# Half-size buffers for raw weights, later places for the stores of early-made weights, and a wider spread of the early parts

## The chip, the cores and the metric

The kernel runs on one core of a Trainium2 chip. The metric is device time in microseconds (us), the median of three runs. Lower is better. In the trace PE is TensorE, PEld its weight loads, DVE VectorE, ACT ScalarE, POOL GpSimd and SP SyncE, the engine whose queue issues nearly all transfers.

## The reference, cut to what matters

Two layers of a diffusion backbone work on 256 context tokens and 256 latent tokens of width 1024. Layer 0 mixes tokens by retention with four heads, layer 1 by a gated linear recurrence (RG-LRU). Each layer then has a gated convolutional feed-forward block (FFN). All norms are modulated by vectors that come from two large products with `ada_w`.

```python
for i in range(DEPTH):                       # DEPTH = 2
    mod_l = (silu_c @ ada_w[i] + ada_b[i])   # six vectors of 1024 for each sequence
    h_l, h_c = modulate(rmsnorm(x, ...)), modulate(rmsnorm(ctx, ...))
    out_c, out_l = retention_mixer(...) if i == 0 else lru_mixer(...)
    x, ctx = x + g1 * out_l, ctx + cg1 * out_c
    x = x + g2 * conv_ffn(...)               # (silu(conv(h @ w_up)[:2816]) * conv(...)[2816:]) @ w_down
    ...                                      # ctx gets its FFN in layer 0 alone
return rmsnorm(x, final_norm)
```

Everything is float32, and each weight is used once: 1888 blocks of 128 x 128 in all.

## The kernel before, in words

**Blocks, units, pieces.** The weights are packed in the order of use. Eight blocks make a unit (128 x 1024, 512 KB), sixteen make a piece (1 MB). Products are made in three passes of a reduced float format: a weight is split into a rounded part `whi` and a rest `wlo`, and `mm3` (L489) multiplies `whi` by the high part of the data, `whi` by its low part, and `wlo` by the high part (L491, L492, L493). So each unit needs one cast on ACT (L392, `whi`) and one subtraction on DVE (L425, `wlo`) before PE can use it. `prep_units` (L376) writes both into the program one to three units ahead of PE. The engines run their instructions in the written order.

**Retention, first FFN, recurrence, second FFN.** Blocks 0 to 511 belong to the retention (four heads; blocks 96 to 127, 224 to 255 and 352 to 383 hold the queries and keys of heads 1 to 3, with their rotation on DVE), 512 to 1039 to the first FFN (up in 512 to 687 and 784 to 951, down in 688 to 783 and 952 to 1039), 1040 to 1359 to the recurrence and 1360 to 1887 to the second FFN.

**Ada pieces.** 40 pieces of `ada_w` are mixed into the stream ("ada"; eight small ones at the start come another way). Most are multiplied by a column on ACT (`adap`, L548) and summed on POOL (`ada`, L549), up to eight products a piece, four of them at each tick.

**Early parts.** The 20 pieces of the recurrence (blocks 1040 to 1359) are not split when they are used. They are loaded, split and stored to memory during the retention and the first FFN, and the recurrence loads the finished halves. Such a part is made by `pre_piece` (L429): two casts on ACT (L442), two subtractions on DVE (L449, with a copy of 32 rows, L452, for some blocks), and two stores of 1 MB, `keep` (L454 to L456). The steps wait in `preq`, and `tick` (L333) puts one step at a time into the program. A tick comes after each group of products, mostly every eight blocks; the two staged stretches, at the borders of the retention, the first FFN and the recurrence, have none.

`PRE = (160, 40)` (L261) says where the parts lie: the n-th at block 160 + 40 n, rounded down to a piece.

**Buffers and the queue.** Raw pieces go into four buffers of 1 MB (L367). A load (L369) is written into SP's queue when the piece before it is begun. There it waits until the piece that had the buffer is split or multiplied. SP issues in order, so what waits at its head holds up everything behind it, the stores (L456) included. Other intermediate tiles share a pool of 56 buffers of 2 KB a partition (L281).

Of the kernel before, what the change touches and what calls it, by code (L numbers as in the profile page):

```python
# [7 lines left out]
F32 = mybir.dt.float32  # L8
# [4 lines left out]
P = 128  # L13
D = 1024
KD = D // P
NT = 512
# [241 lines left out]
            self.issue(t, e, at)  # L258


PRE = (160, 40)  # L261
BLOCKS, PIECES, KEPT = make_plan()
AH = (2, 3, 3)
DI = (3, 2, 8)
SO, SI, SQ = (0, 6, 1.0)
# [7 lines left out]
class Net:  # L273
    def __init__(self, ctx, tc, wpk, xt, cv, par, cst, out):
        self.tc, self.nc, self.out = tc, tc.nc, out
        self.d_w, self.d_x, self.d_c, self.d_par, self.d_cst = wpk, xt, cv, par, cst
        self.cp = ctx.enter_context(tc.tile_pool(name="cp", bufs=1))
        self.wp = ctx.enter_context(tc.tile_pool(name="wp", bufs=WBUFS))
        self.gp = ctx.enter_context(tc.tile_pool(name="gp", bufs=1))
        self.pp = ctx.enter_context(tc.tile_pool(name="pp", bufs=8, space=bass.MemoryType.PSUM))  # L280
        self.nslot = 56  # L281
        self.uid = 0
        self.raw, self.units = {}, {}
        self.npiece = self.nunit = self.nlo = self.pos = self.npast = 0
# [6 lines left out]
        self.preq = deque()  # L291
# [41 lines left out]
    def tick(self, n=1):  # L333
        self.now += 1
        self.sync()
        ready = [f for t, f in self.due if t <= self.now]
        self.due = [(t, f) for t, f in self.due if t > self.now]
        for f in ready:
            f()
        for _ in range(min(self.ada_rate, len(self.adaq))):  # L340
            self.adaq.popleft()[1]()
        if self.preq:
            self.preq.popleft()[1]()
        for _ in range(min(n, len(self.bg))):
            self.bg.popleft()()
# [4 lines left out]
        self.sync()  # L350


    def load_pieces(self, upto):
        while self.npiece <= min(upto, len(PIECES) - 1):
            i = self.npiece
            if PIECES[i][:2] == ("ada", "k"):
                self.raw[i] = [self.slot(name="ak") for _ in range(4)]
                for j, r in enumerate(self.raw[i]):
                    self.nc.sync.dma_start(r, self.d_w[i, :, j * NT:(j + 1) * NT])
                self.npiece += 1  # L360
                continue
            while self.adaq and self.adaq[0][0] <= i - 4:
# [3 lines left out]
            n = PIECE if PIECES[i][0] != "blk" else min(PIECE, (len(BLOCKS) - PIECES[i][1]) * P)  # L366
# [3 lines left out]
            self.raw[i] = r  # L370
            self.npiece += 1
            if cut < n:
                self.load_pieces(i + 1)
                self.nc.sync.dma_start(r[:, cut:n], self.d_w[i, :, cut:n])

    def prep_units(self, upto):  # L376

# [18 lines left out]
    def unit_hi(self, e):  # L396
        u = self.nunit
        if u in KEPT:
            hi, lo = (self.wp.tile([P, UNIT], F32R, tag=f"w{n}", name=f"w{n}{u}") for n in ("hi", "lo"))
            for j, t in enumerate((hi, lo)):  # L400
                self.nc.sync.dma_start(t.bitcast(F32), self.kept[u][:, j, :])
            self.units[u] = (hi.bitcast(F32), hi, lo)
            self.nunit += 1
            return
        pi = self.piece_of[u // 2]
        self.pass_ada(pi)
        self.load_pieces(pi + 1)
        r = self.raw[pi][:, (u % 2) * UNIT:(u % 2 + 1) * UNIT]
# [20 lines left out]
    def pre_piece(self, pi):  # L429

        nc = self.nc
        self.load_pieces(pi + 1)
        r = self.raw[pi]
        st = {}

        def hi(h, u):
            st[h] = t = self.wp.tile([P, 2, UNIT], F32R, tag="pre", name=f"pre{u}", bufs=2)
            o = 0
            cuts = [(a, n) for kind, a, n in self.runs(u) if kind == "main"] + [(UNIT, UNIT)]
            for a, n in cuts:  # L440
                if a > o:
                    nc.scalar.copy(t[:, 0, o:a], r[:, h * UNIT + o:h * UNIT + a])  # L442
                if n > a:
                    nc.scalar.copy(t[:, 0, a:n].bitcast(F32), r[:, h * UNIT + a:h * UNIT + n])
                o = n

        def lo(h, u):
            t = st[h]
            nc.vector.tensor_tensor(t[:, 1, :], r[:, h * UNIT:(h + 1) * UNIT], t[:, 0, :].bitcast(F32), ALU.subtract)  # L449
# [12 lines left out]

    def runs(self, u):

# [61 lines left out]
    def ada_piece(self, pi):  # L526
        _, name, i, half = PIECES[pi]
        layer, bs = ADA_GROUPS[name]
        self.load_pieces(pi + 1)
        r = self.raw[pi]  # L530
        nc = self.nc
        first, last = (i, half) == (0, 0), (i, half) == (len(bs) - 1, 1)
        if first:
# [6 lines left out]
            acc.update({(i, s): self.slot(name="ada") for s in seqs})  # L540

        def product(s, j):
            w, cs = r[:, j * 512:(j + 1) * 512], self.strip[:, half * 4 + j, 30 + s:31 + s]
            if (half, j) == (0, 0):
                nc.scalar.mul(acc[i, s], w, cs)
            else:
                t = self.slot(name="adap")
                nc.scalar.mul(t, w, cs)  # L548
                nc.gpsimd.tensor_tensor(acc[i, s], acc[i, s], t, ALU.add)  # L549

        if name == "g1":
            for j in range(4):
                nc.tensor.matmul(ps[32 * j:32 * j + 32, :], self.strip[:, half * 4 + j, 30 - 2 * i:62 - 2 * i],
                                 r[:, j * 512:(j + 1) * 512], start=first, stop=last, tile_position=(0, 32 * j))
        else:
            self.adaq.extend((pi, lambda s=s, j=j: product(s, j)) for j in range(4) for s in seqs)

        def total(ns):

            for n in ns:  # L560
                (b, s), j = sums[n], n % 4
                o = 30 - 2 * b - s
                nc.tensor.matmul(ps[32 * j:32 * j + 32, :], self.onehot[:, o:o + 32], acc[b, s],
                                 start=n < 4, stop=n >= len(sums) - 4, tile_position=(0, 32 * j))
        if half and name != "g1":
            done = [n for n, (b, s) in enumerate(sums) if b <= i]
            ready = len(sums) if last else len(done) // 4 * 4
            ns = range(self.ada_sum.get(name, 0), ready)
            self.ada_sum[name] = ready
            if ns:  # L570
                self.adaq.append((pi, lambda: self.after(5, lambda: total(ns))))
        if last:
            rows = self.slot(name="adarow")

# [14 lines left out]
            self.adaq.append((pi, lambda: (self.after(n + 1, down), self.after(n + 3, up))))  # L589

    def need(self, name):

# [114 lines left out]
    def setup(self):  # L707
# [13 lines left out]
        self.load_pieces(1)  # L721
        nc.sync.dma_start(self.par[:, 112:], self.d_par[:, 112:])
        self.load_pieces(10)
# [1034 lines left out]
```

## Time and profile before

| | |
|---|---|
| median of 3 runs | 1257.3 us (1255.05 to 1258.12) |
| the profiled execution | 1258.7 us, its span 1256.9 us |
| PE busy | 1196.5 us (95% of the span), 6760 matmuls |
| DVE, ACT, POOL busy | 887.3, 728.9, 352.6 us |
| bytes moved | 265.3 MB, 211 GB/s over the span |
| the chain that ended last | PE 64%, DVE 14%, ACT 9%, DMA 8% |

Times in the trace start at the span's first instruction. PE counts as busy while a matmul is under way, at whichever clock; the granted clock stands as PEclk in the view by stretches, 1.00 for the full 2.4 GHz and 0.50 for 1.2 GHz. The time of a stretch on PE is therefore read from the number of its matmuls, not from its busy share alone.

### The profile page before, as it was taken

What the parts mean: (1) busy time and instruction counts of PE and PEld (TensorE: products, weight loads), DVE (VectorE), ACT (ScalarE), POOL (GpSimd) and SP (SyncE); (2) the same over time, 40 slices, a digit from 0 to 9 for tenths busy, and PEclk for the clock granted to TensorE, in tenths of its full rate; (3) what the DMA queues carried; (4) which work ended last, traced back from release to release, by engine and by line L of the source; (5) the groups of instructions that cost most, each with busy time, mean ns of one, the idle gap of its engine ahead of it and who ended that gap; (6) DMA issues with size and microseconds to landing.
All of it is one profiled execution on the core that took longest, in us unless ns stands there. A gap on an engine that the chain in (4) does not pass through costs nothing.

```text
span 1256.9 us, 17610 instructions
## 1 busy us (share of the span) xinstructions
PE 1196.5 (95%) x6760; PEld 1014.0 (81%) x6760; DVE 887.3 (71%) x1285; ACT 728.9 (58%) x1098; POOL 352.6 (28%) x242
## 2 busy tenths in 40 slices
PE   8999899989989999988899999899999999999997
PEld 4778688768778888776678887678988889999996
DVE  5655966977595688798864576743757967988843
ACT  5345556656754446767745566532487865766642
POOL 0000546557350021588745344312000001000010
PEclk9999999999999999989999999999999999999999
DMA  9851266656355345576687777622677785455541
GB/s 329 304 186 68 101 248 242 210 217 257 127 205 226 125 186 202 204 264 238 239 326 267 268 268 286 249 101 75 211 279 244 283 306 195 167 177 193 197 140 34
DMA packets 50789, 265.34 MB, mean 211 GB/s; under 512 B 6160, under 2 KB 9872, under 8 KB 25488
## 3 DMA queue, kind: packets, MB, share of 16 engines
q1 hardware_dynamic: 50128, 263.69, 57.4%
q8 instruction: 53, 0.87, 0.3%
q10 hardware_dynamic: 576, 0.52, 0.1%
q14 instruction: 32, 0.26, 0.1%
HBM read 219.62 MB, written 42.99 MB: 209 GB/s over the span
## 4 chain that ended last, share of the span: by engine, by line
PE 64%; DVE 14%; ACT 9%; DMA 8%; issue 3%; SPq 1%; POOL 0%; DVEq 0%; ACTq 0%
PE ps L491 17%; PE ps L493 17%; PE ps L492 17%; DMA raw<-wpk 7%; DVE wlo L425 3%; ACT adap L548 3%; PE ps L915 2%; PE ps L916 2%; PE ps L917 2%; DVE pre L449 2%; ACT whi L392 1%; PE av L492 1%; PE av L491 1%; PE av L493 1%; DVE rstd L648 1%
## 5 line engine op out<-in xcount | busy, mean ns | idle before, releaser
L549 POOL TENSOR_TENSOR ada<-ada,adap 128x512 f32<-128x512 f32 x196 | 312.7, 1619 | 384.9 <-ACT adap L548 356.0
L425 DVE TENSOR_TENSOR wlo<-raw,whi 128x1024 fp32r<-128x1024 f32 x196 | 276.7, 1416 | 31.5 <-ACT whi L392 31.3
L392 ACT CAST whi<-raw 128x1024 fp32r<-128x1024 f32 x196 | 203.4, 1043 | 160.0 <-DMA raw<-wpk 136.5
L493 PE MATMUL ps<-hhi,wlo 128*128 128x512 f32 (+1 forms) x640 | 248.3, 388 | 26.3 <-DVE wlo L425 26.3
L491 PE MATMUL ps<-hhi,whi 128*128 128x512 f32 (+1 forms) x640 | 251.0, 392 | 0.0
L492 PE MATMUL ps<-hlo,whi 128*128 128x512 f32 (+1 forms) x640 | 246.7, 385 | 0.3 <-DVE hlo L667 0.3
L634 POOL TENSOR_TENSOR sq<-sq,sq 128x256 f32<-128x256 f32 x33 | 36.4, 1111 | 496.9 <-ACT sq L628 496.5
L492 PE MATMUL ps<-hx,whi 128*128 128x256 f32 x592 | 168.1, 284 | 0.4 <-DVE hx L667 0.2
L491 PE MATMUL ps<-hx,whi 128*128 128x256 f32 x592 | 168.2, 284 | 0.1
L493 PEld LDWEIGHTS ps<-hhi,wlo 128*128 128x128 f32 x640 | 123.0, 192 | 55.2 <-DVE wlo L425 31.6
L493 PE MATMUL ps<-hx,wlo 128*128 128x256 f32 x592 | 167.5, 283 | 0.0
L491 PEld LDWEIGHTS ps<-hhi,whi 128*128 128x128 f32 x640 | 122.9, 192 | 30.9 <-issue 5.3
L492 PEld LDWEIGHTS ps<-hlo,whi 128*128 128x128 f32 x640 | 123.0, 192 | 24.1 <-issue 1.0
L548 ACT ACTIVATE adap<-raw,strip 128x512 f32<-128x512 f32 x196 | 126.0, 713 | 0.0
L491 PEld LDWEIGHTS ps<-hx,whi 128*128 128x128 f32 x592 | 113.5, 192 | 4.1 <-issue 2.5
L492 PEld LDWEIGHTS ps<-hx,whi 128*128 128x128 f32 x592 | 113.5, 192 | 1.1 <-DVE hx L667 0.8
L493 PEld LDWEIGHTS ps<-hx,wlo 128*128 128x128 f32 x592 | 113.6, 192 | 0.0
L1157 DVE SCALAR_TENSOR_TENSOR cv<-ps,par,cv 128x510 f32<-128x510 f32 (+1 forms) x88 | 53.9, 612 | 74.3 <-ACT cv L1154 74.0
L491 PE MATMUL ps<-fzhi,whi 128*128 128x512 f32 (+1 forms) x198 | 73.6, 372 | 2.2 <-ACT fzhi L513 2.2
L1154 ACT ACTIVATE cv<-ps,par 128x512 f32<-128x512 f32 (+1 forms) x88 | 58.5, 666 | 29.1 <-PE ps L493 29.1
L492 PE MATMUL ps<-fzlo,whi 128*128 128x512 f32 (+1 forms) x198 | 73.1, 369 | 0.2 <-DVE fzlo L514 0.2
L493 PE MATMUL ps<-fzhi,wlo 128*128 128x512 f32 (+1 forms) x198 | 73.1, 369 | 0.0
(204 smaller groups left out, 2298.0 us busy)
## 6 DMA issues: line engine op xcount, KB each, us to landing
raw<-wpk SPq DMA_DIRECT2D x157, 1024.0 KB, 5.9
kept<-pre SPq DMA_DIRECT2D x40, 1024.0 KB, 4.9
whi<-kept SPq DMA_DIRECT2D x40, 512.0 KB, 4.5
wlo<-kept SPq DMA_DIRECT2D x40, 512.0 KB, 5.5
ak<-wpk SPq DMA_DIRECT2D x32, 256.0 KB, 6.5
xc<-xt SPq DMA_DIRECT2D x4, 256.0 KB, 4.0
x<-xt SPq DMA_DIRECT2D x4, 256.0 KB, 5.8
raw<-wpk SPq DMA_DIRECT2D x2, 512.0 KB, 6.1
```

The source lines that it names most:

```text
L392: self.nc.scalar.copy(dst, src)
L425: self.eng(e).tensor_tensor(d[q, o:n], r[q, o:n], hi[q, o:n].bitcast(F32), ALU.subtract)
L449: nc.vector.tensor_tensor(t[:, 1, :], r[:, h * UNIT:(h + 1) * UNIT], t[:, 0, :].bitcast(F32), ALU.subtract)
L491: mm(ps, w[0], x[0], start=start, stop=False)
L492: mm(ps, w[0], x[1], start=False, stop=False)
L493: mm(ps, w[1], x[0], start=False, stop=stop)
L548: nc.scalar.mul(t, w, cs)
L549: nc.gpsimd.tensor_tensor(acc[i, s], acc[i, s], t, ALU.add)
L634: nc.gpsimd.tensor_tensor(self.acc[s], self.acc[s], sq, ALU.add)
L915: mm(pss[t], xh, wh, start=k == 0, stop=False)
L1154: nc.scalar.activation(acc, ps[:, :n], AF.Identity, scale=w(1), bias=self.pc("fcb", layer * 44 + f))
L1157: nc.vector.scalar_tensor_tensor(a3[:, :, 1:], p3[:, :, :NS - 1], w(0), a3[:, :, 1:], ALU.mult, ALU.add)
```

## The change

It has three parts.

1. Raw weights come as halves. `make_loads` lists every load as (piece, half); the pool has `RAWS = 9` buffers of 512 KB in place of four of 1 MB, 4.5 MB for 4 MB. `half` writes loads into SP's queue `AHEAD = 2` halves past the one that is begun. A load waits for the half that stood nine halves earlier. To make room the shared pool shrinks from 56 to 54 buffers.
2. `keep` no longer enters the queue with the next step. It goes to `keepq` with a mark two ticks later, and `tick` takes one from there at a time.
3. `PRE` becomes (64, 48): the n-th early part lies at block 64 + 48 n. The first are at blocks 64, 112, 160 and 208 (before: 160, 192, 240, 272), the last is at 976 (before: 912).

```diff
-PRE = (160, 40)
+PRE = (64, 48)
+RAWS, AHEAD = 9, 2
+def make_loads():
+    loads, place = [], {}
+    for i, p in enumerate(PIECES):
+        if p[:2] == ("ada", "k"):
+            loads.append((i, None))
+        else:
+            loads.extend((i, h) for h in range(2) if p[0] != "blk" or p[1] + 8 * h < len(BLOCKS))
...
+LOADS, PLACE = make_loads()
...
-        self.nslot = 56
+        self.nslot = 54
...
+        if self.keepq and self.keepq[0][0] <= self.now:
+            self.keepq.popleft()[1]()
         if self.preq:
             self.preq.popleft()[1]()
...
-            while self.preq and self.preq[0][0] <= i - 4:
+            while any(t <= n - RAWS for t, _ in self.preq):
                 self.preq.popleft()[1]()
-            r = self.wp.tile([P, PIECE], F32, tag="raw", name=f"raw{i}", bufs=4)
-            cut = n if i > 1 else UNIT
-            self.nc.sync.dma_start(r[:, :cut], self.d_w[i, :, :cut])
...
+            r = self.wp.tile([P, UNIT], F32, tag="raw", name=f"raw{pi}{'ab'[h]}", bufs=RAWS)
+            self.nc.sync.dma_start(r, self.d_w[pi, :, h * UNIT:(h + 1) * UNIT])
+            self.raw[pi, h] = r
+
+    def half(self, pi, h, ahead=AHEAD):
+        self.load(PLACE[pi, h][0] + ahead)
+        return self.raw[pi, h]
...
         def hi(h, u):
+            while len(self.keepq) > 1:
+                self.keepq.popleft()[1]()
...
         def lo(h, u):
...
+            self.keepq.append((self.now + 2, lambda: keep(h, u)))
...
-        self.preq.extend((pi, f) for f in (
-            lambda: hi(0, u), lambda: (lo(0, u), hi(1, u + 1)), lambda: (lo(1, u + 1), keep(0, u)),
-            lambda: keep(1, u + 1)))
+        a, b = (PLACE[pi, h][1] for h in range(2))
+        self.preq.extend([(a, lambda: hi(0, u)), (b, lambda: (lo(0, u), hi(1, u + 1))), (b, lambda: lo(1, u + 1))])
```

Where SP's queue held the two stores of an early part one behind the other, it now has loads between them. This is the part at block 640, in the first FFN; before, its tiles are `pre_4955` and `pre_5005`. Of the loads behind the stores the third, `raw_5125`, is the next piece of blocks.

```order
L369 DMA raw_4916<-wpk 128x2048
L369 DMA raw_5015<-wpk 128x2048
L456 DMA kept_5019<-pre_4955 128x2048
L456 DMA kept_5021<-pre_5005 128x2048
L369 DMA raw_5023<-wpk 128x2048
L369 DMA raw_5121<-wpk 128x2048
L369 DMA raw_5125<-wpk 128x2048
L369 DMA raw_5127<-wpk 128x2048
```

The same part in SP's queue after the change. `raw86` is the next piece of blocks behind the first store, `raw89` the next behind the second.

```order
L394 DMA raw85a<-wpk 128x1024
L394 DMA raw85b<-wpk 128x1024
L482 DMA kept_5264<-pre_5104 128x2048
L394 DMA raw86a<-wpk 128x1024
L394 DMA raw86b<-wpk 128x1024
L394 DMA raw87a<-wpk 128x1024
L482 DMA kept_5323<-pre_5156 128x2048
L394 DMA raw87b<-wpk 128x1024
L394 DMA raw88a<-wpk 128x1024
L394 DMA raw88b<-wpk 128x1024
L394 DMA raw89a<-wpk 128x1024
```

Both stores stand further down, and three half loads stand between them.

How far the weights behind a store are from their use shows on ACT. Before, from the second cast of that part to the cast of the blocks behind its store (`raw_5125`):

```order
L442 CAST pre_5005<-raw_4910 128x1024
L513 CAST fzhi_5007<-cv_4905 128x512
L1154 ACTIVATE cv_5010<-ps_4963,par_89 128x512
L392 CAST whi_5025<-raw_5015 128x1024
...
L392 CAST whi_5073<-raw_5015 128x1024
...
L392 CAST whi_5129<-raw_5125 128x1024
```

After, from the same cast on (`raw86` stands behind the first store, whose cast is eight instructions higher, and `raw89` behind the second):

```order
L467 CAST pre_5156<-raw81b 128x1024
L538 CAST fzhi_5158<-cv_5050 128x512
L1179 ACTIVATE cv_5161<-ps_5112,par_89 128x512
L417 CAST whi_5172<-raw84a 128x1024
...
L417 CAST whi_5224<-raw84b 128x1024
...
L417 CAST whi_5282<-raw86a 128x1024
...
L417 CAST whi_5334<-raw86b 128x1024
...
L417 CAST whi_5392<-raw89a 128x1024
```

Counted on ACT, 17 instructions lay between the cast of a stored half and the first cast behind its store; now it is 25 (first store) and 31 (second store).

On DVE a new part comes into the stretch of head 1's queries and keys (blocks 96 to 127). Before, the split of a unit (`wlo`), the readout of head 0 (`zt`, `zlo`) and the rotation (`ra`, `rb`) alternate:

```order
L425 TENSOR_TENSOR wlo_1194<-raw_1007,whi_1128 128x1024
L514 TENSOR_TENSOR zlo_1167<-zt_1163,zhi_1166 128x512
L976 SCALAR_TENSOR_TENSOR zt_1230<-av_1078,par_89,rstd_1160 128x512
L977 TENSOR_TENSOR zt_1230<-zt_1230,sg_775 128x512
L514 TENSOR_TENSOR zlo_1173<-zt_1169,zhi_1172 128x512
```

After, the second subtraction of the part at block 112 stands between them (the first is a dozen rows higher):

```order
L449 TENSOR_TENSOR wlo_1244<-raw21b,whi_1173 128x1024
L539 TENSOR_TENSOR zlo_1215<-zt_1211,zhi_1214 128x512
L474 TENSOR_TENSOR pre_1209<-raw20b,pre_1209 128x1024
L1001 SCALAR_TENSOR_TENSOR zt_1281<-av_1121,par_89,rstd_1205 128x512
L1002 TENSOR_TENSOR zt_1281<-zt_1281,sg_794 128x512
L539 TENSOR_TENSOR zlo_1221<-zt_1217,zhi_1220 128x512
```

Nothing else in that row of work has changed its place.

## Rows read from the trace of the kernel before

**Rows 1.** Waits of PE, 125 to 812 us: total us, times, longest

```profile
PE ps L493 <- DVE wlo L425: 37.4, 16, 5.2
```

**Rows 2.** View by stretches: length, busy us (instructions) of PE, PEld, DVE, ACT, POOL; PEclk, DMA share, GB/s

```profile
125.00:160.00 35.00, 31.30 (x131) 24.28 (x130) 34.38 (x53) 21.18 (x35) 21.10 (x13) 0.95 0.31 103
...
250.00:280.00 30.00, 24.43 (x100) 19.32 (x99) 21.97 (x36) 15.89 (x25) 13.52 (x9) 0.94 0.59 221
...
344.00:372.00 28.00, 24.30 (x99) 19.36 (x99) 27.27 (x36) 14.85 (x26) 20.26 (x12) 0.94 0.59 215
...
526.00:632.00 106.00, 88.25 (x351) 68.98 (x350) 88.36 (x72) 74.35 (x112) 85.78 (x53) 0.92 0.64 239
632.00:660.00 28.00, 27.24 (x114) 21.25 (x115) 17.20 (x19) 14.48 (x20) 11.55 (x8) 0.94 0.80 314
660.00:775.00 115.00, 114.83 (x508) 93.69 (x507) 72.87 (x87) 67.51 (x94) 53.97 (x35) 1.00 0.72 273
775.00:812.00 37.00, 32.46 (x138) 25.11 (x137) 21.71 (x22) 22.78 (x33) 15.40 (x11) 0.95 0.74 287
```

**Rows 3.** Waits of ACT, 160 to 830 us

```profile
ACT whi L392 <- DMA raw<-wpk: 132.9, 28, 11.3
```

**Rows 4.** Waits of SP's queue, 160 to 830 us

```profile
SPq L456 <- DVE pre L449: 151.1, 25, 24.5
SPq L369 <- ACT adap L548: 134.9, 26, 12.3
SPq L456 <- DVE pre L452: 77.5, 12, 14.0
```

**Rows 5.** Instructions of SP's queue in order of time: start, us from first to last

```profile
539.37 4.14 SPq L456 DMA_DIRECT2D kept<-pre  x2
543.60 3.14 SPq L369 DMA_DIRECT2D raw<-wpk  x3
```

**Rows 6.** Chain of waits, 240 to 275 us: start, us, what

```profile
242.55 0.33 SPq L456
...
243.40 8.96 DMA raw<-wpk
```

**Rows 7.** Waits of ACT in 250:280, 344:372, 526:632 and 775:812

```profile
ACT whi L392 <- DMA raw<-wpk: 14.5, 2, 9.2
...
ACT whi L392 <- DMA raw<-wpk: 2.9, 1, 2.9
...
ACT whi L392 <- DMA raw<-wpk: 19.6, 7, 4.2
...
ACT whi L392 <- DMA raw<-wpk: 13.0, 2, 8.0
```

**Rows 8.** Waits of DVE, 526 to 632 us

```profile
DVE cv L1157 <- ACT cv L1154: 18.1, 5, 5.7
```

**Rows 9.** DVE lines L425, L449, L452: ns least/median/most, first and last start

```profile
L425 DVE TENSOR_TENSOR wlo<-raw,whi x196: 1160/1218/2329, 19.0 to 1233.4; 128x1024 fp32r<-128x1024 f32 x196
...
L449 DVE TENSOR_TENSOR pre<-raw,pre x40: 1211/1222/2354, 160.0 to 791.9; 128x1024 fp32r<-128x1024 f32 x40
...
L452 DVE CAST pre<-pre x16: 278/1250/1377, 263.4 to 640.8; 32x256 fp32r<-32x256 f32 x16
```

**Rows 10.** Issue to landing, L369 (raw loads, 1 MB) and L401 (finished halves, 512 KB)

```profile
DMA to landing us min/median/max: 4.7/5.8/13.9
...
DMA to landing us min/median/max: 3.7/5.2/10.0
```

**Rows 11.** View by stretches, the start and the middle of the recurrence

```profile
0.00:31.40 31.40, 26.64 (x124) 14.62 (x128) 17.55 (x35) 17.25 (x29) 1.68 (x11) 1.00 0.94 329
...
1005.52:1036.90 31.38, 29.58 (x216) 25.92 (x215) 21.91 (x40) 21.82 (x35) 0.00 (x0) 0.99 0.89 305
```

More of the change, by code (lines that the diff above doesn't have):

```diff
@@ L258, in run @@
             self.issue(t, e, at)
-PRE = (160, 40)
+PRE = (64, 48)
+RAWS, AHEAD = 9, 2
 BLOCKS, PIECES, KEPT = make_plan()
+def make_loads():
[5 more added lines that the diff above has]
+            loads.extend((i, h) for h in range(2) if p[0] != "blk" or p[1] + 8 * h < len(BLOCKS))
+    a = loads.index((1, 1))
+    loads.insert(a + 1, loads.pop(a))
+    n = 0
+    for i, (pi, h) in enumerate(loads):
+        place[pi, h] = (i, n)
+        n += h is not None
+    return loads, place
+LOADS, PLACE = make_loads()
 AH = (2, 3, 3)
@@ L350, in flush, with load @@
         self.sync()
[L353 to L360, printed above, removed]
+    def load(self, upto):
+        while self.nload <= min(upto, len(LOADS) - 1):
+            pi, h = LOADS[self.nload]
+            self.nload += 1
+            if h is None:
+                self.raw[pi] = [self.slot(name="ak") for _ in range(4)]
+                for j, r in enumerate(self.raw[pi]):
+                    self.nc.sync.dma_start(r, self.d_w[pi, :, j * NT:(j + 1) * NT])
                 continue
-            while self.adaq and self.adaq[0][0] <= i - 4:
+            n = PLACE[pi, h][1]
+            while any(t <= n - RAWS for t, _ in self.adaq):
                 self.adaq.popleft()[1]()
-            while self.preq and self.preq[0][0] <= i - 4:
+            while any(t <= n - RAWS for t, _ in self.preq):
                 self.preq.popleft()[1]()
-            n = PIECE if PIECES[i][0] != "blk" else min(PIECE, (len(BLOCKS) - PIECES[i][1]) * P)
-            r = self.wp.tile([P, PIECE], F32, tag="raw", name=f"raw{i}", bufs=4)
-            cut = n if i > 1 else UNIT
-            self.nc.sync.dma_start(r[:, :cut], self.d_w[i, :, :cut])
[L370 to L374, printed above, removed]
+            r = self.wp.tile([P, UNIT], F32, tag="raw", name=f"raw{pi}{'ab'[h]}", bufs=RAWS)
[4 more added lines that the diff above has]
+        return self.raw[pi, h]
     def prep_units(self, upto):
@@ L406, in unit_hi @@
         self.pass_ada(pi)
-        self.load_pieces(pi + 1)
-        r = self.raw[pi][:, (u % 2) * UNIT:(u % 2 + 1) * UNIT]
+        r = self.half(pi, u % 2)
         hi = self.wp.tile([P, UNIT], F32R, tag="whi", name=f"whi{u}")
@@ L431, in pre_piece @@
         nc = self.nc
-        self.load_pieces(pi + 1)
-        r = self.raw[pi]
+        rs = [self.half(pi, h) for h in range(2)]
         st = {}
         def hi(h, u):
+            while len(self.keepq) > 1:
+                self.keepq.popleft()[1]()
             st[h] = t = self.wp.tile([P, 2, UNIT], F32R, tag="pre", name=f"pre{u}", bufs=2)
-            o = 0
+            r, o = rs[h], 0
             cuts = [(a, n) for kind, a, n in self.runs(u) if kind == "main"] + [(UNIT, UNIT)]
@@ L528, in ada_piece @@
         layer, bs = ADA_GROUPS[name]
-        self.load_pieces(pi + 1)
-        r = self.raw[pi]
+        rs = [self.half(pi, h) for h in range(2)]
+        places = [PLACE[pi, h][1] for h in range(2)]
         nc = self.nc
@@ L553, in ada_piece @@
                 nc.tensor.matmul(ps[32 * j:32 * j + 32, :], self.strip[:, half * 4 + j, 30 - 2 * i:62 - 2 * i],
-                                 r[:, j * 512:(j + 1) * 512], start=first, stop=last, tile_position=(0, 32 * j))
+                                 rs[j // 2][:, j % 2 * 512:(j % 2 + 1) * 512], start=first, stop=last, tile_position=(0, 32 * j))
         else:
-            self.adaq.extend((pi, lambda s=s, j=j: product(s, j)) for j in range(4) for s in seqs)
+            self.adaq.extend((places[j // 2], lambda s=s, j=j: product(s, j)) for j in range(4) for s in seqs)
         def total(ns):
@@ L570, in ada_piece @@
             if ns:
-                self.adaq.append((pi, lambda: self.after(5, lambda: total(ns))))
+                self.adaq.append((places[1], lambda: self.after(5, lambda: total(ns))))
         if last:
@@ L588, in ada_piece @@
             n = 0 if name == "g1" else 5
-            self.adaq.append((pi, lambda: (self.after(n + 1, down), self.after(n + 3, up))))
+            self.adaq.append((places[1], lambda: (self.after(n + 1, down), self.after(n + 3, up))))
     def need(self, name):
@@ L720, in setup @@
         self.load_const("sel")
-        self.load_pieces(1)
+        self.load(3)
         nc.sync.dma_start(self.par[:, 112:], self.d_par[:, 112:])
-        self.load_pieces(10)
+        self.load(LOADS.index((10, None)))
         self.mod = [self.const([P, 48, 2], name="mod") for _ in range(2)]
```

12 lines of the change are left out of this document (6 added, 6 removed).

## The prediction

> **What bounds the kernel now.** I read the page first: PE is busy for 95% of the span, so a change that adds no matmul can win back only what PE loses. The waits of PE between 125 and 812 us, where raw weights, ada pieces and early parts come together, have one large row: 37.4 us in 16 waits, all for `wlo`, the subtraction on DVE [rows 1]. The reader is to see that PE hardly waits for anything else there.
>
> The view by stretches then tells where, and how much it is worth. From 660 to 775 us PE makes 508 matmuls in 115 us at full clock, 0.226 us each; that is PE's own pace. Six stretches fall short of it [rows 2]. Their matmuls at that pace, taken from their length, leave: 125 to 160, 131 matmuls, 29.7 us, 5.3 lost; 250 to 280, 100, 22.6 us, 7.4 lost; 344 to 372, 99, 22.4 us, 5.6 lost; 526 to 632, 351, 79.5 us, 26.5 lost; 632 to 660, 114, 25.8 us, 2.2 lost; 775 to 812, 138, 31.2 us, 5.8 lost. That is 53 us, more than the 37 us of waits, since the granted clock falls to half for a while around each stall (mean 0.92 to 0.95 in these stretches, 1.00 in the full one).
>
> Next, why `wlo` is late. ACT's waits have 132.9 us in 28 waits for a raw load to land before the cast that `wlo` needs [rows 3]. SP's queue says why those loads start late: for 228 us (151.1 and 77.5) its head is a store that waits for an early part's subtraction or row copy, and for 134.9 us a load whose buffer still waits for ACT's ada products [rows 4]. In order of time the pattern is plain: two stores, and right behind them three loads at once [rows 5]. The chain of waits runs through one such place: the store at 242.55, a load from 243.40 that takes 8.96 us because it shares the DMA engines with the store and its neighbours [rows 6]. A load alone lands in 4.7 us [rows 10].
>
> Not all of the loss is of this kind. From 125 to 160 us DVE is busy for 34.4 of 35 us, from 344 to 372 for 27.3 of 28 [rows 2]: there DVE itself is the limit, and ACT waits for loads only 2.9 us in the second of them [rows 7].
>
> **The change part by part.**
>
> *Later stores.* They remove nothing; 40 stores still pass through SP. But before, 17 ACT instructions lay between the cast of a stored half and the first cast that needs a load behind its store; now 25 and 31. A store waits for a subtraction made about one tick after the cast. In the first FFN a tick is eight blocks, 24 matmuls, 5.4 us at full pace. So the head start of the loads goes from about one tick to two or more, 5 us to 11 us or more, against the 7 to 9 us that a load in such a bunch takes [rows 6, 10]. Its bunch is smaller too: the first piece of blocks behind the stores had two whole pieces ahead of it; now there is none behind the first store, and three halves behind the second. I expect most of ACT's waits for loads behind stores to go.
>
> *Halves.* A load waits for the half nine back instead of the whole piece four back: at least one half more of depth, and an ada piece gives back its first half one tick before its second. The loads gated by ada products (134.9 us of SP's waits) start one to two ticks sooner by this. The price: twice as many loads, each issued in about 0.33 us [rows 6] by a queue that mostly waits, so hidden. What a half costs on the DMA engines no raw load shows; the finished halves that the recurrence loads are of that size. Least time alone is 3.7 us against 4.7 for a whole piece [rows 10], so two halves cost between nothing more, if they overlap fully, and 2 x 3.7 - 4.7 = 2.7 us a piece, if not at all. By carried bytes, the recurrence's halves go at 305 / 0.89 = 343 GB/s of full share [rows 11], whole pieces with stores at 314 / 0.80 = 392 [rows 2], 14% less. At 0.64 to 0.80 share that binds nowhere in the middle; at the start the share is 0.94, and pieces 4 and 8 come there: 0 to 5.4 us; nearest to the measured rates, I take 0.5. The Trainium skill speaks against this edit: its page "DMA: Bandwidth & Descriptors" (Rules for kernel authors) asks for at least 1 MiB a transfer, and by its fixed 2.0 us a transfer (Anatomy of one DMA, measured on another issuing path) each halved piece would take 2 us more; by that rule the 0.5 would be 4 for pieces 4 and 8. The trace agrees for a transfer alone, where half the bytes save only 1 us of 4.7, and not at the rates of full queues.
>
> *54 shared buffers for 56.* No wait of ACT for a POOL sum shows in the trace, so 0; if buffers run out in the first FFN, ACT waits for POOL, which is busy 85.8 of 106 us there [rows 2]: at most that stretch then keeps its length.
>
> *Wider parts.* DVE's sum of work stays. Two things move. In blocks 240 to 288 one part is left where two were, and with them two subtractions and two row copies, 2 x 1.2 + 2 x 1.25 = 5 us by the medians [rows 9], leave DVE in and just before 250 to 280. And the part now at block 112 puts two subtractions into 125 to 160, where DVE is full: 2 x 1.21 to 2 x 2.35 us [rows 9], and PE waits for DVE there, so it is on the path. I take 3.0 (2.4 to 4.7, up to 1.75 more for a clock drop: 5% of 35 us). The part at block 352 has one row copy more than before: +1.25 in 344 to 372, which ACT's 2.9 us there offset: 0 (-3 to +3). In the first FFN's up stretch three parts stay three; only the last slides by a piece.
>
> *Now the gains.* 526 to 632: ACT's 19.6 us of waits for loads [rows 7] stand behind DVE's 18.1 us of waits for ACT [rows 8]. If all go, DVE is next: 88.4 us of work, and at the 97 to 98% that its fullest rows show, 91 us. So between 91 and 106; with a few us of idling left I take 93, a gain of 13. 250 to 280: DVE has only 22.0 us of work and loses 5, PE needs 22.6; 14.5 us of waits for loads [rows 7] go: gain 5.5 of the 7.4 (3 to 7.4). 775 to 812: DVE 21.7, PE 31.2, waits for loads 13.0: gain 5.0 of 5.8 (2 to 5.8). 632 to 660 is the tail of the stretch before: 1 (0 to 2).
>
> *Sum:* +0.5 + 3.0 + 0 - 13 - 5.5 - 5.0 - 1.0 = -21. The profiled execution took 1258.7 us, so 1237.7; it lay 1.4 above the median of 1257.3, so 1236 for the median. With the good ends (0 + 2.4 - 3 - 15.4 - 7.4 - 5.8 - 2 = -31) it is 1226; with the poor ones of the middle terms (2 + 4.7 + 1 - 8 - 4 - 3 = -7) 1250.
>
> **Rivals.**
>
> *VectorE keeps the first FFN.* DVE's subtractions take 2.3 us instead of 1.2 at many places [rows 9], POOL is busy 81% of 526 to 632, and a faster stretch has both at once more often. Then the 13 us and the 1 us stay lost: -7, time 1250. For it: 88 of 106 us busy already. Against: DVE's idle time has ACT, and ACT's has loads, as its releaser [rows 7, 8].
>
> *The stores still stand first.* They still wait for the same subtractions at the head of one queue, and loads behind them are still bunched. If DVE runs a tick late just where parts lie, the second tick is eaten and only the depth gained by halves stays: about -2, time 1255. Against: 25 and 31 instructions for 17.
>
> *Slower: the full DVE stretches grow.* Place: 125 to 160 and 344 to 372. Price: two slowed subtractions 4.7, one copy 1.4, and a further clock drop in each, 1.75 twice: +9.6. It decides as soon as the other stretches give back under 9 us, so when loads after stores stay as late as now; then 1267 less the 1.4: about 1265. For it: both rows are at 97 to 98%. Against: the stretches that follow have room on DVE (22.0 of 30 us, 72.9 of 115 in rows 2).
>
> *Halves overlap badly.* Each pair costs the 2.7 us that the landing times allow at most. Pieces 4 and 8 then add 5.4 at the start, and a load behind a store loses about half of its second tick, so half of the 24.5 us of gains stays lost: 5.4 + 3 - 12 = -4, time 1253. For it: rows 10; against: rows 2 and 11, by bytes. The page's rule of 1 MiB points this way.
>
> *PE at its own pace.* With fewer stalls POOL's and DVE's slow pairs part, and nearly all 53 us but the DVE-full stretches' come back: about 1218.
>
> **How the numbers follow.** Forecast 1236, chance 0.55 (1226 to 1250). VectorE keeps the first FFN, 1250: 0.16. Stores still first, 1255: 0.08. Halves overlap badly, 1253: 0.04. Slower, 1265: 0.10. PE's pace, 1218: 0.07. A measurement of this kernel tells 0.3%, some 3.8 us, from no change: faster is below 1253.5, same up to 1261. From the cases: faster 0.55 + 0.07 + 0.14 + 0.02 + 0.03 = 0.81, same 0.02 + 0.06 + 0.01 + 0.01 = 0.10, slower 0.09. The range that leaves out a tenth on either side is 1220 to 1256.
>
> **What would show it.** Right: ACT's waits for raw loads from 160 to 830 us fall from 133 us to under 50; SP's waits at the stores shrink, and loads no longer follow them three at once; PE's waits for `wlo` fall from 37 to under 22 us; 351 matmuls of the first FFN's up stretch take about 93 us, with DVE at 93% or more; the first stretch around 125 us is some 3 us longer; raw halves land in about 4 us. The forecast is wrong if ACT's waits go and the up stretch still takes over 100 us (first rival), if ACT's waits stay above 100 us (second), or if the early stretches lose more than the later ones give back (third).

## The result, and the profile after

The changed kernel takes 1240.8 us (median of 4 runs, 1239.3 to 1242.0) against 1257.7 us (4 runs, 1255.1 to 1258.9) for the kernel before, timed beside it: a ratio of 0.9868, 95% interval 0.9848 to 0.9888. The forecast was 1236 in 1220 to 1256. The profiled execution took 1242.0 us, its span 1240.2, so 16.7 us less than the one before.

On the page, the busy line has PE at nearly the same busy time in a shorter span, and the line of the chain has DMA at 4% where it had 8, ACT at 3 where it had 9:

```profile
PE 1190.2 (96%) x6760; PEld 1012.2 (82%) x6760; DVE 899.3 (73%) x1285; ACT 730.9 (59%) x1098; POOL 365.5 (29%) x242
...
PE 74%; DVE 15%; DMA 4%; issue 3%; ACT 3%; SPq 1%; POOL 0%; DVEq 0%; ACTq 0%; POOLq 0%
```

PE's waits from 125 to 800 us (total us, times, longest) answer to [rows 1]. The 37.4 us for `wlo` are 20.0 now; two waits that were small have grown, the second and the third row (2.4 and 2.2 us before, shown behind them):

```profile
PE ps L518 <- DVE wlo L449: 20.0, 9, 6.0
PE st L663 <- POOL sq L659: 4.7, 2, 4.1
PE ps L516 <- ACT fzhi L538: 4.1, 1, 4.1
```

```profile
PE st L638 <- POOL sq L634: 2.4, 2, 1.7
PE ps L491 <- ACT fzhi L513: 2.2, 1, 2.2
```

The view by stretches holds the same matmuls as [rows 2], found by their number in the order of PE, so the lengths compare directly (us; busy us of PE, PEld, DVE, ACT, POOL; PEclk, DMA share, GB/s):

```profile
125.14:163.74 38.60, 31.67 (x132) 24.71 (x131) 38.10 (x55) 21.22 (x35) 21.17 (x13) 0.91 0.49 163
...
527.79:622.18 94.39, 82.91 (x351) 65.84 (x349) 92.56 (x72) 69.46 (x104) 86.39 (x50) 0.95 0.75 253
622.18:650.00 27.82, 27.82 (x114) 21.56 (x115) 15.77 (x18) 16.37 (x22) 17.13 (x11) 0.91 0.87 304
650.00:764.38 114.38, 114.38 (x508) 93.88 (x507) 74.72 (x87) 69.30 (x96) 54.50 (x34) 1.00 0.80 278
764.38:794.62 30.24, 30.24 (x137) 24.10 (x136) 24.66 (x26) 18.46 (x26) 15.44 (x9) 1.00 0.72 245
```

The up stretch of the first FFN went from 106 to 94.4 us, and DVE is busy for 98% of it instead of 83%: it has become DVE's stretch. DVE's own work there grew too, from 88.4 to 92.6 us for the same 72 instructions. The last one went from 37 to 30.2 us, all PE. The first one grew from 35 to 38.6 us.

ACT's waits from 160 to 830 us answer to [rows 3]: one row of 132.9 us has become six of one wait each, 17.3 us in all (7.3 + 3.3 + 2.4 + 2.0 + 1.5 + 0.8). The first two:

```profile
ACT whi L417 <- DMA raw29a<-wpk: 7.3, 1, 7.3
ACT whi L417 <- DMA raw96a<-wpk: 3.3, 1, 3.3
```

DVE's waits from 526 to 625 us answer to [rows 8], 18.1 us there. This row is all that is left:

```profile
DVE fzlo L539 <- ACT fzhi L538: 0.8, 1, 0.8
```

SP's queue (160 to 830 us) answers to [rows 4]. The waits at stores, L482, fall from 228.6 to 138.2 us; 19.0 us more now stand at loads that wait for a part's subtraction. The largest row is loads that wait for a buffer which DVE gives back in its normal course:

```profile
SPq L394 <- DVE wlo L449: 297.5, 81, 16.6
SPq L482 <- DVE pre L474: 104.6, 19, 27.6
SPq L394 <- ACT adap L573: 93.8, 43, 11.0
SPq L482 <- DVE pre L477: 33.6, 11, 10.9
SPq L394 <- DVE pre L474: 19.0, 11, 3.6
```

That row was the largest before the change as well, though [rows 4] do not show it:

```profile
SPq L369 <- DVE wlo L425: 223.3, 41, 18.4
```

And the same early part as in [rows 5], in order of time: two stores there and three loads of 1 MB in a bunch behind them. Now each store stands between half-size loads, which go out a few us apart:

```profile
538.17 0.33 SPq L482 DMA_DIRECT2D kept<-pre  x1
538.59 0.38 SPq L394 DMA_DIRECT2D raw79a<-wpk  x1
540.87 0.33 SPq L394 DMA_DIRECT2D raw79b<-wpk  x1
542.64 0.33 SPq L394 DMA_DIRECT2D raw80a<-wpk  x1
543.02 0.42 SPq L482 DMA_DIRECT2D kept<-pre  x1
543.54 0.40 SPq L394 DMA_DIRECT2D raw80b<-wpk  x1
```

Where the 16.7 us lie is read from the start of the same-numbered matmul in the two traces. The table has it for every kernel that ran; a cell is by how much a stretch (named by its times in the kernel before) is longer than before, the last one up to the start of the last matmul. The two kernels with squares to PE have four matmuls more, which are left out of the count.

| kernel, profiled execution | 0-120 | 120-235 | 235-322 | 322-470 | 470-512 | 512-673 | 673-838 | rest | sum |
|---|---|---|---|---|---|---|---|---|---|
| **the change** | +0.1 | +3.6 | -5.7 | +0.7 | +3.1 | -11.8 | -7.4 | +0.7 | -16.7 |
| later stores alone | +0.6 | 0 | -2.0 | +1.5 | 0 | +0.1 | +5.3 | 0 | +5.5 |
| wider parts alone | +7.0 | +7.6 | -5.6 | 0 | +1.6 | +5.8 | -6.8 | -1.5 | +8.0 |
| halves alone | -0.1 | +0.7 | +0.5 | -0.4 | +3.8 | +10.9 | -5.3 | -1.4 | +8.8 |
| stores and wider parts | +0.2 | +2.7 | -5.5 | +1.0 | +0.1 | +1.3 | -7.4 | 0 | -7.6 |
| halves and stores | +2.0 | +0.7 | -3.4 | +0.8 | -0.8 | -6.4 | -7.4 | 0 | -14.5 |
| halves and wider parts | +1.3 | +4.9 | -5.8 | -0.5 | +5.6 | -7.3 | -7.4 | -1.4 | -10.6 |
| the change, ring of eight | -0.5 | +2.7 | -5.5 | +0.8 | +2.9 | -11.4 | -7.4 | 0 | -18.4 |
| the change, part at 96 | -0.2 | +1.4 | -5.7 | +0.7 | +3.0 | -11.8 | -7.4 | +0.1 | -20.0 |
| the change, squares to PE | -0.3 | +3.5 | -5.7 | 0 | -1.4 | -12.7 | -7.4 | +0.1 | -23.7 |
| the change, parts by hand | -0.6 | +0.7 | -5.7 | +0.7 | +1.8 | -24.7 | -7.4 | 0 | -35.1 |
| the same, squares to PE | 0 | +0.8 | -7.3 | 0 | -0.9 | -24.7 | -7.4 | 0 | -39.6 |
| before, parts by hand | +6.6 | +4.8 | -6.9 | 0 | +2.0 | -12.3 | -7.4 | 0 | -13.2 |

### The profile page after: what moved, and what is told of

It is laid out like the page before. It is cut to its first block, busy times and chain, and to the rows that moved or that the text cites. A ratio compares the mean times of both kernels' runs of the same rounds, so it can differ in the third digit from the quotient of the medians.

```text
span 1240.2 us, 17983 instructions
## 1 busy us (share of the span) xinstructions
PE 1190.2 (96%) x6760; PEld 1012.2 (82%) x6760; DVE 899.3 (73%) x1285; ACT 730.9 (59%) x1098; POOL 365.5 (29%) x242
## 3 DMA queue, kind: packets, MB, share of 16 engines
q1 hardware_dynamic: 72736, 263.70, 61.9%
## 4 chain that ended last, share of the span: by engine, by line
PE 74%; DVE 15%; DMA 4%; issue 3%; ACT 3%; SPq 1%; POOL 0%; DVEq 0%; ACTq 0%; POOLq 0%
PE ps L516 21%; PE ps L517 20%; PE ps L518 20%; DVE wlo L449 4%; PE ps L940 2%; PE ps L941 2%; PE ps L942 2%; DVE pre L474 1%; DVE zlo L539 1%; PE av L517 1%; PE av L516 1%; PE av L518 1%; DVE fzlo L539 1%; DVE cv L1182 1%; DVE zt L1001 1%
## 5 line engine op out<-in xcount | busy, mean ns | idle before, releaser
L574 POOL TENSOR_TENSOR ada<-ada,adap 128x512 f32<-128x512 f32 x196 | 323.3, 1674 | 351.3 <-ACT adap L573 212.4
L518 PE MATMUL ps<-hhi,wlo 128*128 128x512 f32 (+1 forms) x640 | 245.8, 384 | 13.3 <-DVE wlo L449 13.3
L659 POOL TENSOR_TENSOR sq<-sq,sq 128x256 f32<-128x256 f32 x33 | 38.7, 1181 | 500.9 <-ACT sq L653 500.4
L516 PEld LDWEIGHTS ps<-hhi,whi 128*128 128x128 f32 x640 | 122.3, 191 | 31.4 <-issue 4.9
L702 DVE SCALAR_TENSOR_TENSOR xc<-ps,mod,xc 128x256 f32<-128x256 f32 x48 | 23.0, 479 | 60.9 <-PE ps L518 60.9
L518 PE MATMUL ps<-zhi,wlo 128*128 128x512 f32 (+1 forms) x152 | 55.9, 368 | 6.7 <-DVE wlo L449 6.7
L517 PE MATMUL ps<-zlo,whi 128*128 128x512 f32 (+1 forms) x152 | 55.7, 366 | 2.6 <-DVE zlo L539 2.6
```

The source lines that it names most:

```text
L516: mm(ps, w[0], x[0], start=start, stop=False)
L517: mm(ps, w[0], x[1], start=False, stop=False)
L518: mm(ps, w[1], x[0], start=False, stop=stop)
L659: nc.gpsimd.tensor_tensor(self.acc[s], self.acc[s], sq, ALU.add)
```

## The experiments

Each was timed beside the kernel before; times are medians, ratios are to the kernel before with their 95% interval.

**Each edit by itself.** Later stores alone, in the whole-piece kernel:

```diff
+        if self.keepq and self.keepq[0][0] <= self.now:      # in tick
+            self.keepq.popleft()[1]()
...
+            self.keepq.append((self.now + 2, lambda: keep(h, u)))   # in lo
```

> The kernel before with the later stores alone (whole pieces in four buffers, 56 shared buffers, parts at 160 + 40 n). Theory (loads held up behind the stores were the loss): ACT's waits for raw loads fall from 133 us to under 70 and the time to about 1246 (-10 to -14), without the +3.6 us that the part at block 112 costs. Rival (the halves do it, by their depth): the time stays at 1255 to 1258.

Measured: 1262.5 us, 1.0042 (1.0028 to 1.0055), 0.4% slower where a gain was expected. SP's waits from 160 to 830 us (total us, times, longest) show what became of the wait; L461 is the store, L371 the load:

```profile
SPq L371 <- ACT adap L552: 176.1, 34, 13.1
SPq L371 <- DVE pre L453: 109.2, 15, 25.8
SPq L461 <- DVE pre L453: 21.8, 6, 11.8
SPq L461 <- DVE pre L456: 10.9, 3, 6.0
```

The waits at stores did collapse, 228.6 to 32.7 us. But the load four pieces behind an early part takes that part's own raw buffer, and that comes back with the part's second subtraction: the event that the store waited for. So 109.2 us of the wait only changed its instruction; the rest came up at other loads, which wait 41 us longer for ada products and 53 us longer for `wlo`. ACT still waits 115.2 us for raw loads. The loss itself lies at 673-838 (+5.3); what makes loads late there was not followed.

Wider parts alone:

```diff
-PRE = (160, 40)
+PRE = (64, 48)
```

> The kernel before with the parts at 64 + 48 n alone. Theory: stores stand where they stood, so ACT's waits for loads stay above 100 us; +3.6 us at 125 us for the part at block 112, some 3 us back near 250 us where two parts become one, so 1256 to 1261. Rival (the spread thins out VectorE's work and that is the gain): 1243 to 1248.

Measured: 1269.4 us, 1.0099 (1.0083 to 1.0114), slower, 8 us above the expected range. It keeps the gains at 235-322 and 673-838. At 120-235 it loses 7.6 us, and the matmuls at 512 to 526 take 24.2 us for 13.8, where ACT waits 15.8 us for two raw loads. It also loses 7 us ahead of 120, where PE (waits from 60 to 125 us) stands still for an ada piece whose load is held up behind the store of the part at block 64:

```profile
PE ada L553 <- DMA raw<-wpk: 4.9, 1, 4.9
```

ACT's waits for raw loads, 160 to 830 us, are 97.7 us, less than the 132.9 before, in a slower kernel: their sum alone does not tell the time.

Halves alone (each store right behind its subtraction, old places):

```diff
-            self.keepq.append((self.now + 2, lambda: keep(h, u)))
+        self.preq.extend([..., (b, lambda: (lo(1, u + 1), keep(0, u))), (b, lambda: keep(1, u + 1))])
```

> The halves alone: nine half buffers, loads two halves ahead, 54 shared buffers; stores follow with the next step as before, parts at 160 + 40 n. Theory: loads still stand behind the stores, but in smaller bunches and one half deeper: 1247 to 1253, ACT's waits for loads 60 to 100 us. Rival (halves by depth do it all): 1241 or less.

Measured: 1268.5 us, 1.0093 (1.0079 to 1.0107), slower. SP in order of time, at the early part at 520 us: the second store holds the queue until 532, all buffers come free meanwhile, and seven halves go out in 5 us:

```profile
521.53 10.99 SPq L481 DMA_DIRECT2D kept<-pre  x2
532.57 0.42 SPq L394 DMA_DIRECT2D raw74a<-wpk  x1
533.04 0.91 SPq L394 DMA_DIRECT2D raw74b<-wpk  x1
534.00 1.02 SPq L394 DMA_DIRECT2D raw75a<-wpk  x1
535.12 0.67 SPq L394 DMA_DIRECT2D raw75b<-wpk  x1
```

ACT's longest wait for a raw load in any of these runs follows (waits of ACT, 500 to 550 us):

```profile
ACT whi L417 <- DMA raw75a<-wpk: 15.8, 1, 15.8
```

With shorter waits for buffers SP reaches the stores sooner and stands there longer: its waits at stores from 160 to 830 us rise to 306.8 us (208.8 and 98.0), while those at loads for `wlo` fall from 223.3 to 126.3. My theory, by which stores alone bring most of the gain and halves some, fell with these runs.

**Two edits at a time.** Stores and wider parts, without halves (the first two diffs above together):

> The change without the halves: later stores and parts at 64 + 48 n, whole pieces in four buffers. Theory: most of the gain is there without halves, 1241 to 1247; what is left to the halves is the loads that wait for ada products. Rival (halves by depth): 1254 or more.

Measured: 1251.7 us, 0.9963 (0.9950 to 0.9975), between the theory's range and the rival's. The places keep their gain (-5.5 and -7.4), and the later stores spare the 7 us at the ada piece; the up stretch does not move (+1.3), and ACT still waits 106.2 us for loads from 160 to 830 us. Halves and stores, with the parts at the old places:

```diff
-PRE = (64, 48)
+PRE = (160, 40)
```

> The changed kernel with its early parts at the places of before (every 40 blocks from block 160); halves in nine buffers and later stores stay. Theory (two gates in series hold the loads: a store at the head of SP's queue that waits for its part's second half, and the ring of raw buffers; each edit alone only moves the wait to the other gate): with both gates wider ACT's waits for raw loads fall from 136 us to below 40 us and the kernel takes 1236 to 1248 us; the parts at the old places keep the losses at 250-280 and 775-812 us of the kernel before, or some of them. Rival (the gain is the places of the parts): over 1252 us, with ACT's waits above 80 us.

Measured: 1243.3 us, 0.9890 (0.9877 to 0.9904); ACT's waits for raw loads are 28.2 us over the whole run (136.5 before), each over 0.3 us counted. At these places that is what two gates in series do: either edit alone costs time, both together gain. Halves and wider parts, each store right behind its subtraction (the third diff above, with the wider places):

> The changed kernel with each store issued where it was before, in the background step right behind its subtraction; halves and the wider spread stay. Theory (two gates): the store gate is still there and halves make SP wait at it no less, so ACT's waits for raw loads stay above 80 us and the kernel takes 1256 to 1272 us. Rival (the nine half buffers and the places of the parts bring the gain, the later stores nothing): 1240 to 1246 us, ACT's waits below 40 us.

Measured: 1247.2 us, 0.9923 (0.9910 to 0.9937), ACT's waits 75.1 us. Here the theory missed: with SP's waits at stores as long as with halves alone (184.0 + 113.8 = 297.8 us), the kernel is 9.5 us faster than before. In the matmuls at 512 to 639 us of the kernel before, ACT's waits for raw loads are 14.6 us against 26.4 with halves alone. That run and this one differ in the places alone, so with halves the wider places are worth 21 us; by which waits, no run separates.

With this run every combination of the three edits has been timed:

| median, us | neither | later stores | halves | both |
|---|---|---|---|---|
| places of before | 1257 | 1262.5 | 1268.5 | 1243.3 |
| wider places | 1269.4 | 1251.7 | 1247.2 | 1240.8 |

At the old places either edit alone costs 5 to 12 us. At the wider places, where the kernel without them is slower, either alone brings some 18 or 22 us, and the second adds 6 to 11. Two gates that have to open together describe the old places only.

**Ring of eight halves**, as many bytes as the four pieces of before:

```diff
-RAWS, AHEAD = 9, 2
+RAWS, AHEAD = 8, 2
...
-        self.nslot = 54
+        self.nslot = 56
```

> The changed kernel with eight half buffers in place of nine, which is as many bytes as the four whole buffers of the kernel before; the two buffers of the general pool that this frees go back to it. It tells whether the gain is the finer steps of the ring or its larger size. Theory (finer steps: a buffer comes back after each half, not after each piece): 1240 to 1245 us, ACT's waits for raw loads below 45 us. Rival (the ninth buffer carries the gain): over 1247 us, ACT's waits above 70 us.

Measured: 1240.9 us, 0.9874 (0.9854 to 0.9894), no difference from nine; ACT's waits for raw loads are 31.4 us over the whole run against 21.5. What halves add to later stores and wider parts (1251.7 to 1240.9) needs no ninth buffer and no more bytes; the ring's finer step carries it, together with how far ahead loads are written, which changed with it.

**The two losses that the change made.** The second early part at block 96 in place of 112 (here and below the places are a list, of which the n-th is the n-th part's):

```diff
-PRE = (64, 48)
+PRE = (64, 96, 160, 208, ...)
```

> The changed kernel with its second early part at block 96 in place of block 112; all other parts stay. Theory (the stretch 125-160 us has no idle VectorE, and the part's two subtractions there make PE's weights late): the stretch returns to the length it had before the change, the wait for the low weights of 6.0 us at 145 us falls to about 3 us, and the kernel is 3 to 4 us faster than the changed one, about 1237 us. Rival (the low weights are late there in any case, and the part at block 96 delays something else): within 1 us of the changed kernel's 1241 us.

Measured: 1239.4 us, 0.9860 (0.9847 to 0.9874), not told apart from the change by the time. The trace shows the sign right and the size too large: +1.4 instead of +3.6 at 120-235, PE's wait 3.7 us instead of 6.0. The last two squares of the statistics straight to PE, without POOL's addition:

```diff
         self.need("f0")
-        self.stats_begin()
+        self.stats_begin(2)
```

> The changed kernel in which the last two squares ahead of the retention's statistics go to PE each by itself, so that the last POOL addition of two squares is left out of the chain. Theory (that addition took 4.2 us beside three back-to-back VectorE subtractions, against 1.9 us before the change, and PE waited 4.1 us for it): the wait at 480 us goes, the cumulative loss of 3.2 us there with it, and the kernel is 3 to 4 us faster than the changed one, about 1237 us. Rival (PE would then wait as long for the squares themselves or for the statistics behind them, or the half clock comes all the same): within 1 us of the changed kernel.

Measured: 1236.2 us, 0.9833 (0.9817 to 0.9849). The +3.1 at 470-512 became -1.4, as the theory had it: PE waits for no addition there any more (no row from 460 to 505 us).

**Places by hand**, which take two parts (640 and 688) out of the up stretch:

```diff
-PRE = (64, 48)
+PRE = (64, 96, 160, 208, 240, 320, 352, 400, 432, 464, 496, 544, 592, 720, 752, 784, 832, 880, 928, 976)
```

> The changed kernel with the twenty early parts placed by hand: at 96 in place of 112, two out of the first feed-forward's up blocks (640 and 688 go; 432, 752 and others come in where VectorE has idle time), 256 and 304 go to 240 and 320. Theory (a part's two subtractions and casts, 5.9 to 7.3 us of VectorE in the up stretch, lengthen a stretch in which VectorE is full by part of that, and cost nothing where it has idle time): the stretch at 120-160 us gives 1.5 us, 250-284 us 2 us, the up stretch 6 to 9 us; 1229 to 1234 us. Rival (parts closer together, 32 blocks apart, bring the stores and loads into each other's way again and make PE wait in the stretches of before): 1238 to 1245 us, ACT's waits for raw loads above 60 us.

Measured: 1223.0 us, 0.9727 (0.9708 to 0.9745), better than expected. The 351 matmuls of the up stretch, by stretches:

```profile
523.05:607.05 84.00, 80.65 (x351) 65.32 (x350) 78.88 (x64) 66.19 (x100) 80.37 (x47) 0.98 0.68 218
```

DVE has 78.9 us of work where it had 92.6, the stretch takes 84.0 us where it took 94.4. Two parts fewer are 13.7 us less on DVE, 6.8 us a part (12.2 us of it their own subtractions and row copies), and three quarters of that came off the time. With the parts go their loads and stores, which this run does not separate from DVE's work. The 2 us expected at 250-284 did not come: 235-322 stays at -5.7. With the squares straight to PE as well (both diffs):

> Both: the parts placed by hand and the last two squares straight to PE. Theory (the two losses lie in different stretches and add): the parts' gain and 4 to 6 us beside it, 1224 to 1231 us, faster than every kernel so far. Rival (the wait at 480 us came from how the parts fell there, so moving them takes it away too): the same as the kernel with the parts alone, within 1 us.

Measured: 1219.8 us, 0.9702 (0.9684 to 0.9721), the fastest of all; 3% below the kernel before. The squares bring 3.1 us here, less than the 4 to 6 expected: with the parts by hand only +1.8 was left at 470-512.

**The same places in the kernel before**, with whole pieces and stores as they were (only the list):

> The kernel before (whole pieces in four buffers, stores where they were) with nothing changed but the list of places of the twenty early parts, the one that took the changed kernel from 1241 to 1223 us. It tells whether places alone carry what the change and the list brought together. Theory (halves, later stores and places are needed together in the up stretch: with whole pieces and stores at the head of SP's queue VectorE still waits there for ACT and ACT for loads): 1240 to 1258 us, ACT's waits for raw loads above 80 us, the up stretch at most 8 us shorter than before. Rival (VectorE's work in its full stretches is all of it, and the change to the loads brings nothing that better places do not bring): 1222 to 1232 us, the up stretch 20 us shorter or more.

Measured: 1246.3 us, 0.9925 (0.9910 to 0.9939). The time is the theory's, and so are ACT's waits for loads (160 to 830 us):

```profile
ACT whi L392 <- DMA raw<-wpk: 107.4, 28, 12.1
```

The step behind it is not. By stretches, the matmuls that stood at 512 to 526 and the 351 of the up stretch, with ACT's waits in the second:

```profile
518.76:544.43 25.67, 16.95 (x63) 13.43 (x61) 10.75 (x11) 15.78 (x24) 12.38 (x9) 0.80 0.64 235
544.43:628.92 84.49, 80.98 (x351) 65.31 (x350) 81.69 (x65) 69.20 (x104) 79.97 (x48) 0.98 0.62 222
ACT whi L392 <- DMA raw<-wpk: 4.3, 2, 2.8
```

The up stretch is 21.5 us shorter than before, as the rival had it, and nearly as short as with the changed loads (84.0). ACT waits 4.3 us for loads in it, where it waited 19.6 us. So in that stretch the two causes do not add: the change takes 11.6 us off it, the list 21.5, both 22.0. What whole pieces cost lies ahead of it: the 25.7 us above were 13.8 in the kernels before and after the change (so the table has -12.3 for 512-673), and parts that begin at block 64 cost 6.6 us ahead of 120 and 4.8 up to 235. With halves and later stores these three are 13.8, -0.6 and +0.7. In the whole time the change alone brings 1.3%, the list alone 0.8%, both 2.7%: more than the sum.

## Why the prediction was right

**The waits.** ACT's waits fell from 133 to 17 us (under 50 forecast), PE's for `wlo` from 37.4 to 20.0 (under 22), SP's at stores from 229 to 138, and the loads left their bunch. The up stretch's 351 matmuls took 94.4 us with DVE at 98% (93 us, 93% or more).

**The terms.** The start was +0.5 and measured +0.1. The part at block 112: +3.0, measured +3.6, with PE's wait grown from 2.9 to 6.0 us there. 250 to 280: -5.5, measured -5.7. 344 to 372: 0, measured +0.7. The up stretch and its tail: -14, measured -11.8; the tail gave nothing: its granted clock has a mean of 0.91, since PE waits 4.1 us for `fzhi` just ahead of it, behind DVE's last up work with the slid part's second subtraction and row copies. With the parts by hand, where that part lies elsewhere, the wait is gone and the tail takes 25.8 us. 775 to 812: -5.0, measured -7.4 from 673 to 838, beyond the 5.8 that the prediction had as most; it priced the 138 matmuls at 31.2 us, and they took 30.2. These sum to -20.5, against -21, in part because the misses on the last two cancel, which is luck. The up stretch fell short since DVE's work there did not stay at 88.4 us.

**The term that was missing** is +3.1 at 470 to 512, most of what lies between -20.5 and -16.7. PE waits there for the last addition of squares on POOL, L659. The prediction has no term for it. It followed the moved parts into two stretches, and not the one at block 496, whose second subtraction now stands among the splits beside that addition (last section). With halves and later stores at the old places the addition takes 1.85 us and 470-512 loses nothing (-0.8). The run with squares to PE shows that PE's wait for it was this loss.

**The step that failed** is the one that gave the gain to single edits: "I expect most of ACT's waits for loads behind stores to go", said of later stores, with halves as a bit more depth. Each of the three edits alone makes the kernel slower, by 0.4 to 1%, and with later stores alone ACT's waits stay at 115 us. A load had two conditions in series, SP's queue past the store and a free buffer, and for a load four pieces behind a part both are the same subtraction. I counted ACT's instructions between a stored half's cast and the first cast behind its store, 17 against 25 and 31, and never asked when that load's buffer comes back. The largest of SP's waits, 223.3 us at loads whose buffer waits for `wlo`, is missing from [rows 4] and from the argument. The forecast came out since all three edits were in it: for this step that is luck.

**The rivals.** *VectorE keeps the first FFN* was half true: DVE is the limit there now, with more work than before as the rival said, but at 94 us, not 106. *The stores still stand first* was priced at 1255; the run with halves and wider parts is nearest to it and took 1247.2. *Halves overlap badly* did not happen, though one sign of mine was wrong: a raw half lands in 5.7 us (median; 3.5 to 12.9), not in about 4, hardly sooner than a whole piece in [rows 10]:

```profile
DMA to landing us min/median/max: 3.5/5.7/12.9
```

[rows 10] hold two raw loads of 512 KB, which the prediction overlooked (median 6.1 us), and 343 against 392 GB/s is 12.5% less, not 14. The DMA engines are busier for the same bytes: with halves alone the packets of SP's queue take 59.9% of 1266.1 us against 57.4% of 1256.9, 5% more, in 72736 packets for 50128. It costs no time that shows: two halves are under way together and ahead of need, and the start is at +0.1. The Trainium skill's rule of 1 MiB, on "DMA: Bandwidth & Descriptors" (Rules for kernel authors), did not decide here: with later stores or wider parts, halves gain. Alone they are slower, and the longest wait there comes from the queue's order, as the seven loads in a bunch show; how much of the loss that is, no run separates.

## What to carry to other kernels

Where a queue that issues in order also feeds a ring of buffers, list for each late transfer both what stands ahead of it and when its buffer returns; opening one gate alone can move the wait to the other, or bunch the transfers, and cost time, as later stores and halves each did at the old places. When waits for loads go, read which engine fills the stretch next, and move work that is not due (here 6.8 us of DVE for each early part) out of that stretch: this brought 18 us on top of the change to the loads, and 10.5 us without it. Name a stretch by its own matmuls: the column 512-673 takes in 14 us ahead of the up stretch, and so hides that the places alone shorten the up stretch as much as both.

## What the runs showed of the hardware

One addition on POOL (128 x 256) took 4.18 us beside three subtractions on DVE without a gap; the run's other 32 took 0.72 to 1.83 us. POOL and DVE after the change, in order of time (start, us):

```profile
474.34 0.74 POOL L659 TENSOR_TENSOR sq<-sq,sq 128x256 f32<-128x256 f32 x1 [1.73 <-ACT sq L653]
475.46 4.18 POOL L659 TENSOR_TENSOR sq<-sq,sq 128x256 f32<-128x256 f32 x1 [0.38 <-ACT sq L653]
```

```profile
475.57 1.22 DVE L449 TENSOR_TENSOR wlo<-raw67a,whi 128x1024 fp32r<-128x1024 f32 x1
476.71 1.22 DVE L474 TENSOR_TENSOR pre<-raw64b,pre 128x1024 fp32r<-128x1024 f32 x1
477.84 1.22 DVE L449 TENSOR_TENSOR wlo<-raw67b,whi 128x1024 fp32r<-128x1024 f32 x1
```

It ends at 479.64, 0.6 us after the third of them. The middle one is that of the early part at block 496. The three other runs with halves, parts at 496 and three subtractions there (halves and wider parts, ring of eight, part at 96) have the same 4.18 us. Before the change one subtraction stood at this place and DVE then waited 0.84 us for ACT; POOL's addition took 1.91 us. With halves at the old places (with and without later stores) it took 1.85 us beside two: the second starts 0.07 us after its cast on ACT has ended, and lasts 1.75 us for 1.2. So the part's subtraction took away the moment at which POOL had come in. The Trainium skill has a rule for it on "SBUF — State Buffer" (Who interferes with whom): a DVE instruction with two inputs in SBUF and a GpSimd instruction that reads SBUF exclude each other. The trace agrees on POOL's side. It shows the other side as well: the same subtraction of DVE takes at most 1.33 us in all 138 cases without POOL work beside it, and each of the 50 that took over 2.0 us (up to 2.35) has POOL work beside it for more than half its time; many lie in the up stretch, where POOL is busy for 86 of 94 us.
